# Weight tiles of 1056 words in place of 1040, and a constant of 64 words in place of 48, in a two-block transformer kernel

## The chip, the cores and the metric

The kernel runs on one core of one Trainium2 chip. The metric is device time in microseconds (us) of one execution, the median of several runs. The core has a matrix engine (PE, with a separate record PEld for its weight loads), a vector engine (DVE), a scalar engine (ACT), a general engine (POOL) and an engine that issues DMAs (SP).

## The reference

Two transformer blocks over 256 tokens of 2048 features, all in 32-bit floating point. What takes the time are the products with weight matrices; the attentions, norms and the modulation stand between them.

```
def first_block(x, ...):
    h = rmsnorm(x, pre_mix_g[l])
    proj = h @ w_in[l]                       # 2048 x 4368
    ...                                      # windowed and forgetting attention
    mix = concatenate([o_a, o_b]) @ w_out[l] # 2048 x 2048
    x = x + rmsnorm(mix, post_mix_g[l])
    u = causal_dwconv(rmsnorm(x, pre_ffn_g[l]) @ w_up[l], conv_w[l], conv_b[l])  # 2048 x 11264
    gate, val = split(u, 2)
    y = (gelu(gate) * val) @ w_down[l]       # 5632 x 2048
    x = x + rmsnorm(y, post_ffn_g[l])

def second_block(x, c, ctx, ...):
    ...                                      # modulation: silu(c) @ w_ada, 2048 x 12288
    q, k, v, u = split_projection(h @ w_in)  # 2048 x 2560; keys and values of ctx too
    x = x + g_a * (concatenate([attn, pool]) @ w_out)
    x = x + g_m * (square(relu(hm @ w_mlp_up)) @ w_mlp_down)  # 2048 x 8192 and back
    return rms_norm(x, final_norm_w)
```

## The kernel before

Every product streams its weight matrix once from memory. `run` walks over blocks of two weight tiles. A raw tile of 32-bit words arrives by DMA (`raw`), ACT rounds it into a tile `hi` (L156), and DVE subtracts to get the remainder `lo` (L168). The resident operand (x^T, features on partitions) lies in memory as `hi` and `lo` parts too, in tiles of the pools `a8` (names a8_...) and `p4` (p4_...). Each product of a weight tile and an x^T tile is made of three matmuls on the rounded 32-bit type: hi with hi, hi with lo, lo with hi.

`products` (the matmul is at L285) knows two forms. In form A the weights are the stationary operand (128 columns of them, loaded ahead of the matmul) and x^T is the moving one, 256 columns. In form B it is the other way round: 128 columns of x^T are stationary and 512 columns of the weights move (352 or 336 in the product `v`, 256 in part of `kv` and `ckv`). Form A makes up, mup, qk, qa, q, kva and half of kv and ckv: 9120 matmuls of 256 columns. Form B makes dn, mdn, wo_a, wo_b, wo2_p, wo2_a and u: 3552 matmuls of 512 columns. The product v (288) and the rest of kv and ckv (192) complete the 13152 matmuls of L285. A **unit** here is the work on one weight tile of 1024 words: 8 feature tiles of 3 matmuls in form A (24), 4 of 3 in form B (12). In a profile row, a name like b_up<-a,hi says: result bank of product up, moving operand from pool a8, stationary operand hi.

The weight tiles come from the pool `w`, four buffers for `hi` and four for `lo`. All tiles lie in one address space of bytes per partition, one pool after the other; the constants (pool `cst`) lie ahead of `raw`, `w`, `a8`, `p4`, `row` and `p2`. The width of 1040 words is set by the product v, the widest. A weight tile of 1040 words takes 4160 bytes, which is 32.5 times 128, so buffers alternate between starts that are multiples of 128 bytes and starts 64 bytes past one. The constant `heads` takes 192 bytes (1.5 times 128), after which everything starts 64 bytes past a multiple of 128. In the built program the first bytes are these (the remainder mod 256 in brackets; slices inside a tile are multiples of 512 bytes in form A and B, so they change nothing in it):

```
                     before                                  after
hi, in order of use  63424 [192] 75904 [128] 71744 [64] 67584 [0]    63488 [0] 76160 [128] 71936 [0] 67712 [128]
lo, in order of use  80064 [192] 92544 [128] 88384 [64] 84224 [0]    80384 [0] 93056 [128] 88832 [0] 84608 [128]
a8 (eight of 8192)   96704 [192], all eight [192]                    97280 [0], all eight [0]
p4 (nine of 4096)    162240 [192], all nine [192]                    162816 [0], all nine [0]
```

Of the kernel before, what the change touches and what calls it, by code (L numbers as in the profile page):

```python
# [9 lines left out]
F32R = mybir.dt.float32r  # L10
# [4 lines left out]
D = 2048  # L15
T = 256
# [5 lines left out]
# columns of the packed per-feature vectors  # L22
# [9 lines left out]
# when the adaptive modulation takes a step, by product: every so many ticks (99: never), or at these ticks  # L32
# [4 lines left out]
# products without a reader while the norms before these products run  # L37
# [3 lines left out]
class Group:  # L41
    """One weight-streaming product: blocks of two 128-row weight tiles against a resident x^T."""
# [10 lines left out]
def a_banks(nf, col0=0):  # L53
    """Feature-major results: two 128-feature tiles of 256 tokens per bank."""
    return [[("A", 256 * j, col0 + 128 * (i + j)) for j in range(min(2, nf - i))] for i in range(0, nf, 2)]


def b_banks(widths, col0=0):
    """Token-major results: one bank per token tile and column chunk."""
    out = []  # L60
    for tt in range(2):
        c = col0
        for n in widths:
            out.append([("B", 0, n, tt, c)])
            c += n
    return out


class Kernel:
# [51 lines left out]
    def run(self, groups):  # L121
        nc = self.nc
        blocks = [(g, b) for g in groups for b in range(g.nb)]
# [24 lines left out]
        def hi_to(j):  # L148
            while len(his) <= min(j, 2 * len(blocks) - 1):
                dma_to(len(his) // 2 + 2)  # L150
                views, raw, w = part(len(his))
                self.n += 1
                hi = self.w_p.tile([128, 1040], F32R, tag="hi", name=f"hi{self.n}")[:, :w]
                with self.behind("hi"):
                    for h, r in views(hi, raw):
                        nc.scalar.copy(h, r)  # L156
                his.append(hi)

        def lo_to(j):
            while len(los) <= min(j, 2 * len(blocks) - 1):  # L160
                n = len(los)
                hi_to(n)
                views, raw, w = part(n)
                self.n += 1
                lo = self.w_p.tile([128, 1040], F32R, tag="lo", name=f"lo{self.n}")[:, :w]
                with self.behind("lo"):
                    for (l, r), (h, _) in zip(views(lo, raw), views(his[n], raw)):
                        self.dve.tensor_tensor(out=l, in0=r, in1=h.bitcast(F32), op=ALU.subtract)  # L168
                los.append(lo)

        banks = None
        for i, (g, b) in enumerate(blocks):
# [40 lines left out]
            if g.tail and b == g.nb - 2:  # L213
                # the first token tile's results come before the second's
                w2 = []
                for u in range(4):
                    lo_to(2 * i + u)
                    hi_to(2 * i + 3)
                    w2.append((his[2 * i + u], los[2 * i + u]))
                    for n in range(nb // 2):  # L220
                        unit(banks[n], g.banks[n], u)
                    self.tick(False)
                for n in range(nb):
                    if n >= nb // 2:
                        for u in range(4):
                            unit(banks[n], g.banks[n], u)
                    mm = self.mm
                    g.done(n, banks[n])
                continue
# [38 lines left out]
    def behind(self, kind):  # L268
        """Issue order after an instruction of a norm that the next products wait for."""
        q = self.held[kind]  # L270
        return self.tc.issue_after(q.pop(0).ins) if q else nullcontext()
# [31 lines left out]
    def later(self, *steps, every=1):  # L303
        """Run steps one by one at coming ticks."""
        def gen():
            for f in steps:
                for _ in range(every):
                    yield
                f()
        self.sides.append(gen())  # L310

    def keep_warm(self, n, after=None, rhs=None):
        """Products without a reader, so that the tensor engine's clock stays up while it would wait."""
        bk = self.bank("warm")
        rhs = self.vecs[:, 0:512] if rhs is None else rhs
        with self.tc.issue_after(after.ins) if after else nullcontext():
            for _ in range(n):
                self.nc.tensor.matmul(bk[:, 0:rhs.shape[-1]], self.ones, rhs, start=True, stop=True, skip_group_check=True)

    def preload(self, func, after):  # L320
        """Has the scalar engine load the table of a function ahead of its use."""
# [9 lines left out]
    def loader(self, w, k0, c0, n):  # L331
        """Blocks of two k-tiles from row k0 and columns c0:c0+n."""
# [7 lines left out]
    def make_ht(self, src, gain, shift=None):  # L340
        """src(tt, k) -> token-major [128, 128]; gain, shift: per-feature columns."""
# [40 lines left out]
        def head(tt):  # L382
            """The first four k-tiles of one token tile."""
# [18 lines left out]
    def rstd(self, parts, n):  # L402
        """(mean of squares + eps) ** -0.5 from partial sums [128, m]."""
# [14 lines left out]
    def scale_rows(self, x, ss, n=D, out=None, first=False):  # L418
        """x * rstd for a token tile; the first of two on one engine, else shared by two."""
# [12 lines left out]
    def row(self, src):  # L432
        """A vector of D on every partition, in two tiles; returns columns of it."""
# [6 lines left out]
    def attn1(self, jobs, v_of, evac, bias, sink):  # L440
        """jobs: (q, k, j, half, head). Yields once per head."""
# [87 lines left out]
    def o_evac(self, his, los, gain, acc, base=0):  # L529
        """o^T of a head pair: times the group's gain, split, and its squares summed."""  # L530
# [16 lines left out]
    def token_rstd(self, acc, n):  # L547
        """rstd per token [128, 2] from squares summed feature-major [128, 256]."""
# [49 lines left out]
    def row_of(self, cols, tile_=None):  # L598
        """A [128, 2048] tile whose every row is the vector held in columns [128, 16]."""
# [13 lines left out]
    def main(self):  # L613
# [15 lines left out]
        heads = self.const("heads", [128, 48])  # L629
# [29 lines left out]
        # x^T of the first block, one token tile after the other  # L659
# [19 lines left out]
        def silu_rows():  # L679
            """silu of c and c_ctx, each along every partition's row."""  # L680
# [18 lines left out]
        # -- v and forget gates, token-major  # L699
# [63 lines left out]
        # -- k and v of the windowed heads  # L763
# [16 lines left out]
        # -- q of the windowed heads, heads j and j + 8 in one tile  # L780
# [19 lines left out]
        # -- q and k of the forgetting heads, with the windowed attention beside them  # L800
# [27 lines left out]
        # -- output projection: windowed heads, then forgetting heads  # L828
        w_out = a["w_out"]

        def pair_rows(w, r0, n, c0):
            """Rows of k-tile j: 64 of head j, 64 of head j + n, among 2n heads from row r0."""
# [28 lines left out]
        def residual(y, x, r):  # L861
            """x += y * r for one token tile; returns the squares' sums of the new x."""
# [8 lines left out]
        def add_norm(n, half, y, hold):  # L871
            """One result chunk of y: its squares, its gain, and then x += norm(y) and y = norm(x)."""
# [44 lines left out]
        # -- residual + norm, then x^T of the next product  # L917
# [6 lines left out]
        # -- first feed-forward  # L924
# [79 lines left out]
        # context: norm, modulation and its x^T beside the last products  # L1004
# [39 lines left out]
        # -- second block: context keys and values  # L1044
# [9 lines left out]
        def split(x, his, lo):  # L1054
            """hi + lo of x [128, 512], hi by partition halves in two tiles."""
# [5 lines left out]
        def twice(c):  # L1061
            """The high parts of the keys in the other partition half too."""
# [6 lines left out]
        # -- second block: projections of the latent tokens  # L1069
# [20 lines left out]
        def rope(x, his, lo):  # L1090
            """Rotated x [128, 512] (features on partitions, 256 tokens twice), as hi (by halves in two tiles) + lo."""
# [33 lines left out]
        # -- attention over the latent window and the context  # L1125
        def attn2():
            # per half s of the heads: high parts in their own partitions, low parts in the other half
# [141 lines left out]
        # -- output projection of the second block: x += g_a * (...)  # L1269
# [51 lines left out]
        # -- second feed-forward  # L1321
# [27 lines left out]
        def finish(n, half):  # L1349
            """The gain of one chunk of the last norm, and the norm when a token tile is complete."""  # L1350
# [77 lines left out]
def arrays(inp):  # L1428
    """The inputs as the program takes them, and constants that depend on shapes alone."""
# [10 lines left out]
    # the two halves of w's columns c0:c1, side by side by 512  # L1440
# [59 lines left out]
```

## Time and profile before

| | us |
|---|---|
| median of 3 runs | 2158.41 |
| lowest and highest run | 2158.36, 2160.49 |
| span of the profiled execution, first to last instruction | 2159.2 |
| PE busy in it | 2134.7 (99%) |
| PEld busy | 1926.6 (89%) |
| DVE busy | 1578.7 (73%) |
| ACT busy | 1076.4 (50%) |

The span is the profiled execution's own time; it lies 0.8 us above the median of the runs. A matmul's recorded duration reaches over the start of the next one, since matmuls are pipelined; the time that one costs in a stream is the step from its start to the start of the next, and that is read from the starts of rows.

### The profile page before, as it was taken

The page shows a single profiled execution, that of the slowest core. Times are in us where ns is not written, and L with a number is a line of the kernel's source. Part 1 is how long each engine was busy: PE and PEld are TensorE (multiplying, and loading weights), DVE is VectorE, ACT ScalarE, POOL GpSimd, SP SyncE. Part 2 cuts the span into 40 slices and gives each one's busy share as a digit, 9 for nine tenths or more (in the row PEclk, how much of TensorE's full clock was granted, in tenths as well). Part 3 has the DMA queues.
Part 4 walks back from the last instruction along what each step waited for, and adds up shares of the span by engine and source line. Part 5 has one row for each costly group of instructions (what it writes and reads, how often), then busy time and mean ns, then how long its engine had stood idle before and what let it go on. Part 6 is the DMA issues. An engine that isn't in the chain of part 4 may idle for free.

```text
span 2159.2 us, 35018 instructions
## 1 busy us (share of the span) xinstructions
PE 2134.7 (99%) x14342; PEld 1926.6 (89%) x14342; DVE 1578.7 (73%) x2094; ACT 1076.4 (50%) x1557; POOL 38.3 (2%) x58
## 2 busy tenths in 40 slices
PE   8999999999999999999999999999999999999998
PEld 7988877999998999989889878889898998989986
DVE  6777688888689787887899777765656657555476
ACT  5456565555454543544666466354543434434343
POOL 0001010000000000000000000000000000000000
PEclk9999999999999999999999999999999999999999
DMA  8753675667767788787878744855767677565572
GB/s 309 262 191 123 157 230 218 231 244 248 254 216 254 252 298 309 273 310 255 307 259 287 247 139 156 196 175 177 252 200 270 215 246 243 191 194 179 194 233 98
DMA packets 120640, 490.86 MB, mean 227 GB/s; under 512 B 8672, under 2 KB 12576, under 8 KB 107040
## 3 DMA queue, kind: packets, MB, share of 16 engines
q1 hardware_dynamic: 120480, 488.63, 67.0%
q8 instruction: 112, 1.84, 0.3%
q14 instruction: 48, 0.39, 0.0%
HBM read 484.90 MB, written 2.13 MB: 226 GB/s over the span
## 4 chain that ended last, share of the span: by engine, by line
PE 95%; DVE 2%; ACT 1%; DMA 1%; POOL 0%; issue 0%; POOLq 0%; ACTq 0%; SPq 0%; DVEq 0%
PE b_up L285 23%; PE b_mup L285 17%; PE b_mdn L285 16%; PE b_dn L285 11%; PE b_qk L285 4%; PE b_wo_a L285 4%; PE b_u L285 2%; PE b_v L285 2%; PE b_wo_p L285 2%; PE b_qa L285 2%; PE b_q L285 2%; PE b_wo_b L285 2%; PE b_aux L1156 1%; PE b_aux L1199 1%; PE b_aux L1185 1%; PE b_aux L495 1%
## 5 line engine op out<-in xcount | busy, mean ns | idle before, releaser
L168 DVE TENSOR_TENSOR lo<-raw,hi 128x1024 fp32r<-128x1024 f32 (+2 forms) x716 | 850.0, 1198 | 445.7 <-ACT hi L156 444.2
L156 ACT CAST hi<-raw 128x1024 fp32r<-128x1024 f32 (+2 forms) x716 | 729.7, 1029 | 859.8 <-PE b_up L285 218.9
L285 PE MATMUL b_up<-a,hi 128*128 128x256 f32 x2816 | 493.9, 280 | 0.0
L285 PEld LDWEIGHTS b_up<-a,hi 128*128 128x128 f32 x2816 | 430.8, 189 | 0.4
L285 PE MATMUL b_up<-a,lo 128*128 128x256 f32 x1408 | 392.8, 279 | 0.0
L285 PE MATMUL b_mup<-a,hi 128*128 128x256 f32 x2048 | 358.8, 279 | 1.3 <-ACT a L370 1.3
L285 PE MATMUL b_mdn<-hi,p 128*128 128x512 f32 x1024 | 319.9, 393 | 0.0
L285 PEld LDWEIGHTS b_mup<-a,hi 128*128 128x128 f32 x2048 | 312.8, 189 | 2.1 <-ACT a L370 1.6
L285 PE MATMUL b_mup<-a,lo 128*128 128x256 f32 x1024 | 285.4, 279 | 0.0
L285 PEld LDWEIGHTS b_up<-a,lo 128*128 128x128 f32 x1408 | 266.1, 189 | 0.0
L583 DVE SCALAR_TENSOR_TENSOR raw<-raw,srow 128x2048 f32<-128x2048 f32 x96 | 219.4, 2286 | 28.5 <-DMA raw<-in_w_ada 28.3
L285 PEld LDWEIGHTS b_mdn<-hi,p 128*128 128x128 f32 x1024 | 191.7, 188 | 44.2
L285 PE MATMUL b_dn<-hi,p 128*128 128x512 f32 x704 | 220.1, 394 | 0.0
L285 PE MATMUL b_mdn<-lo,p 128*128 128x512 f32 x512 | 201.3, 393 | 0.0
L285 PEld LDWEIGHTS b_mup<-a,lo 128*128 128x128 f32 x1024 | 193.4, 189 | 0.0
L285 PEld LDWEIGHTS b_dn<-hi,p 128*128 128x128 f32 x704 | 131.5, 188 | 30.1
L285 PE MATMUL b_dn<-lo,p 128*128 128x512 f32 x352 | 138.5, 393 | 0.0
L285 PEld LDWEIGHTS b_mdn<-lo,p 128*128 128x128 f32 x512 | 96.3, 188 | 22.2
L285 PE MATMUL b_qk<-a,hi 128*128 128x256 f32 x512 | 94.0, 285 | 0.0
L285 PE MATMUL b_wo_a<-hi,a 128*128 128x512 f32 x256 | 81.1, 398 | 0.0
L285 PEld LDWEIGHTS b_qk<-a,hi 128*128 128x128 f32 x512 | 78.2, 189 | 2.6 <-issue 2.0
L285 PEld LDWEIGHTS b_dn<-lo,p 128*128 128x128 f32 x352 | 66.2, 188 | 15.6 <-DVE lo L168 0.4
(264 smaller groups left out, 2542.0 us busy)
## 6 DMA issues: line engine op xcount, KB each, us to landing
raw<-in_w_ada SPq DMA_DIRECT2D x96, 1024.0 KB, 5.6
raw<-in_w_up SPq DMA_DIRECT2D x88, 1024.0 KB, 5.0
raw<-in_w_mlp_up SPq DMA_DIRECT2D x64, 1024.0 KB, 5.1
raw<-in_w_mlp_down SPq DMA_DIRECT2D x64, 1024.0 KB, 5.7
raw<-in_w_in SPq DMA_DIRECT2D x50, 1024.0 KB, 6.0
raw<-in_w_down SPq DMA_DIRECT2D x44, 1024.0 KB, 6.2
raw<-in_w_out SPq DMA_DIRECT2D x32, 512.0 KB, 6.8
raw<-in_w_out SPq DMA_DIRECT2D x16, 1024.0 KB, 6.1
```

Source lines behind the costliest of these rows:

```text
L156: nc.scalar.copy(h, r)
L168: self.dve.tensor_tensor(out=l, in0=r, in1=h.bitcast(F32), op=ALU.subtract)
L285: self.mm = self.pe.matmul(dst, lhsT, rhs, start=first and n == 0 and m == 0, stop=last and n == len(prog) - 1 and m == 2, skip_group_chec ...
L495: self.pe.transpose(t[:, 128 * m:128 * m + 128], z[:, 1 + 128 * m:129 + 128 * m], self.ident)
L583: self.dve.scalar_tensor_tensor(out=r, in0=r, scalar=1.0, in1=self.srow[0], op0=ALU.mult, op1=ALU.mult, accum_out=self.ada[:, f:f + 1])
L1156: self.pe.matmul(bk[:, 256 * m:256 * m + 256], x, k[:, 512 * m + o:512 * m + o + 256], start=n == 0 and m == 0, stop=n == 1 and m == 1, sk ...
L1185: self.pe.transpose(bk[:, 128 * m:128 * m + 128], z[:, 128 * m:128 * m + 128], self.ident)
L1199: self.pe.matmul(o[64 * s:64 * s + 64, 128 * qt:128 * qt + 128], v[:, c:c + 64], PT[x][:, 128 * kt:128 * kt + 128], start=kt == 0, stop=kt ...
```

## The change

The tiles hi and lo become 1056 words wide (4224 bytes, 33 times 128), of which the same columns are used as before. The constant heads becomes 64 words wide, of which 48 are used. By this every hi and lo buffer and every tile of a8 and p4 begins at a multiple of 128 bytes. No instruction is added, removed or moved on any engine: the orders of the five engines are the same row by row, and so are the shapes. Only start addresses differ. (Comments were taken out besides.)

```
-                hi = self.w_p.tile([128, 1040], F32R, tag="hi", name=f"hi{self.n}")[:, :w]
+                hi = self.w_p.tile([128, 1056], F32R, tag="hi", name=f"hi{self.n}")[:, :w]
...
-                lo = self.w_p.tile([128, 1040], F32R, tag="lo", name=f"lo{self.n}")[:, :w]
+                lo = self.w_p.tile([128, 1056], F32R, tag="lo", name=f"lo{self.n}")[:, :w]
...
-        heads = self.const("heads", [128, 48])
+        heads = self.const("heads", [128, 64])[:, 0:48]
```

## Rows read from the trace of the kernel before

**Rows 1.** The page: busy time by engine, and the clock in 40 slices.

```profile
PE 2134.7 (99%) x14342; PEld 1926.6 (89%) x14342; DVE 1578.7 (73%) x2094; ACT 1076.4 (50%) x1557; POOL 38.3 (2%) x58
...
PEclk9999999999999999999999999999999999999999
```

**Rows 2.** The page: the chain that ended last, share of the span by engine.

```profile
PE 95%; DVE 2%; ACT 1%; DMA 1%; POOL 0%; issue 0%; POOLq 0%; ACTq 0%; SPq 0%; DVEq 0%
```

**Rows 3.** Stretches of up5, dn21, mdn20, qk0, u: length, busy time (x) by engine, PEclk.

```profile
core 0: us, PE busy (x) PEld busy (x) DVE busy (x) ACT busy (x) POOL busy (x), PEclk, DMA share, GB/s
692.20:736.80 44.60, 44.60 (x384) 44.56 (x383) 30.70 (x34) 21.01 (x28) 0.54 (x1) 1.00 0.71 256
670.00:692.00 22.00, 22.00 (x97) 17.84 (x96) 19.03 (x21) 8.08 (x9) 0.00 (x0) 1.00 0.83 302
1702.90:1724.90 22.00, 22.00 (x98) 17.86 (x97) 18.04 (x20) 10.28 (x13) 0.00 (x0) 1.00 0.70 226
122.50:192.80 70.30, 70.30 (x532) 60.44 (x531) 53.74 (x128) 40.11 (x100) 9.23 (x16) 1.00 0.42 143
1215.10:1303.90 88.80, 88.80 (x513) 66.71 (x513) 73.31 (x175) 53.02 (x114) 0.00 (x0) 1.00 0.51 160
```

**Rows 4.** Timeline of PE in up5, form A: start, length, instruction, count.

```profile
714.58 0.40 PE L285 MATMUL b_up<-a,hi 128*128 128x256 f32 x2
714.82 0.28 PE L285 MATMUL b_up<-a,lo 128*128 128x256 f32 x1
714.94 0.40 PE L285 MATMUL b_up<-a,hi 128*128 128x256 f32 x2
...
717.46 0.39 PE L285 MATMUL b_up<-a,hi 128*128 128x256 f32 x2
...
717.80 0.39 PE L285 MATMUL b_up<-a,hi 128*128 128x256 f32 x2
...
720.18 0.39 PE L285 MATMUL b_up<-a,hi 128*128 128x256 f32 x2
...
723.02 0.40 PE L285 MATMUL b_up<-a,hi 128*128 128x256 f32 x2
...
725.76 0.40 PE L285 MATMUL b_up<-a,hi 128*128 128x256 f32 x2
```

**Rows 5.** Timeline of PE in mdn20, form B, same columns.

```profile
1702.88 0.63 PE L285 MATMUL b_mdn<-hi,p 128*128 128x512 f32 x2
...
1705.63 0.63 PE L285 MATMUL b_mdn<-hi,p 128*128 128x512 f32 x2
...
1708.43 0.62 PE L285 MATMUL b_mdn<-hi,p 128*128 128x512 f32 x2
...
1711.22 0.62 PE L285 MATMUL b_mdn<-hi,p 128*128 128x512 f32 x2
...
1713.97 0.63 PE L285 MATMUL b_mdn<-hi,p 128*128 128x512 f32 x2
```

**Rows 6.** Timeline of PE in kv, both forms from one weight tile, same columns.

```profile
1149.27 0.40 PE L285 MATMUL b_kv<-hi,a 128*128 128x256 f32 x2
...
1149.62 0.40 PE L285 MATMUL b_kv<-hi,a 128*128 128x256 f32 x2
...
1155.07 0.39 PE L285 MATMUL b_kv<-a,hi 128*128 128x256 f32 x2
...
1155.41 0.39 PE L285 MATMUL b_kv<-hi,a 128*128 128x256 f32 x2
...
1155.76 0.39 PE L285 MATMUL b_kv<-hi,a 128*128 128x256 f32 x2
...
1156.10 0.39 PE L285 MATMUL b_kv<-hi,a 128*128 128x256 f32 x2
...
1156.43 0.39 PE L285 MATMUL b_kv<-hi,a 128*128 128x256 f32 x2
```

**Rows 7.** Timeline of PE: transposes and a product on unrounded words, same columns.

```profile
1156.78 1.03 PE L353 MATMUL b_aux<-ident,a 128*128 128x128 f32 x8
...
1311.48 7.07 PE L1258 MATMUL b_aux<-p,a 128*128 128x256 f32 x32
```

**Rows 8.** Durations of single instructions at L353 and L1258: count, min/median/max in ns.

```profile
L353 PE MATMUL b_aux<-ident,a x120: 270/272/421, 22.3 to 1463.1; 128*128 128x128 f32 x120
...
L1258 PE MATMUL b_aux<-p,a x32: 379/379/379, 1311.5 to 1318.2; 128*128 128x256 f32 x32
```

## The prediction

> **What bounds the kernel now.** I read the busy times first, then the chain of waits, then the stretches, then the starts of single matmuls. PE is busy for 2134.7 of 2159.2 us and its clock is granted in full (2.4 GHz) in every slice [rows 1]. The chain that ended last is PE for 95% of the span [rows 2]. In the streaming stretches PE never stops, while DVE works for 69 to 87% of the time and ACT for less than half; only the attention stretches qk0 and u come near a limit of DVE (54 of 70 and 73 of 89 us) [rows 3]. So the time is the number of matmuls times the step from one start to the next, and only what changes a step counts. Busy times and durations of single matmuls don't show the step, since they overlap; the starts do.
>
> **What the steps show.** In up5 (form A) four weight tiles follow each other, and the x^T tiles all begin 192 bytes past a multiple of 256. The units of 24 matmuls start at 714.58, 717.46, 720.18, 723.02 and 725.76, so they take 2.88, 2.72, 2.84 and 2.74 us, 11.18 us for the four [rows 4]. Nothing else than the buffers' start addresses follows this pattern: the weights begin at 192, 128, 64 and 0 mod 256 in this order. The two long units have stationary operands that begin 64 bytes past a multiple of 128, the two short ones aligned ones. A step is 120, 113, 118 and 114 ns. In form B (mdn20) the x^T tile is stationary, always off by 64, and the moving weights alternate; the units of 12 start at 1702.88, 1705.63, 1708.43, 1711.22 and 1713.97, so they take 2.75, 2.80, 2.79 and 2.75 us for weights at 192, 128, 64 and 0 [rows 5]. Whether the moving operand is aligned makes no difference of note there (2.775 aligned, 2.77 not).
>
> **Two readings of the same rows.** Before the change x^T is never aligned to 128, so two rules fit form A alike. By the first, each operand's own start counts: a stationary operand at a multiple of 128 is faster. By the second, the distance of the two operands counts: when weights and x^T start an odd multiple of 64 bytes apart the two streams of reads fit between each other, and when they start an even multiple apart (0 or 128 mod 256) they collide. After the change every distance is 0 or 128 mod 256, half of the units each, as in the two long units now; and every start is aligned, as in half of the short units now. The first rule makes the kernel faster and the second makes it slower, by nearly the same amount.
>
> What decides for me is three things. First, the two long units differ, 2.88 at distance 0 and 2.84 at distance 128 [rows 4], though their stationary operands have the same start mod 128; an own start mod 128 can't do this, a distance can. Second, kv works on one weight tile in both forms. With weights at 0 its form A steps (x^T moving) take 0.34 us per three matmuls (1155.07 to 1155.41), and form B, in which the misaligned x^T is now the stationary operand, has steps of 0.34 and 0.33 just behind (1155.76 to 1156.10 to 1156.43) [rows 6]. By a rule on the stationary operand alone these should be the 0.36 of the long units. The distance is odd in both. Third, in form B the moving operand's start does nothing [rows 5], where a rule of own starts with a price for each operand would show it. Against it: another unit of kv has form B steps of 0.35 at an odd distance (1149.27 to 1149.62) [rows 6], so the distance is not all; and no row has both operands aligned.
>
> At this place a rule of the Trainium skill speaks against both readings. TensorE: Matmul & The Clock Gate, section Step-by-step: what each phase is for, says that PE has two independent read ports, one for the moving operand and one for LDWEIGHTS, and that loading the next weights doesn't steal read bandwidth from the running matmul. By that rule the place of the operands would be free and the sum of this change zero, 2159 us. The trace disagrees: units alike in all but addresses take 2.88 and 2.72 us [rows 4].
>
> **The sum, by the distance.**
> - Form A: 9120 matmuls are 380 units. The mean unit now is 11.18/4 = 2.795 us. After, half have distance 0 and half 128: (2.88 + 2.84)/2 = 2.86 us. 380 x 0.065 = +24.7 us.
> - Form B of 512 columns: 3552 matmuls are 296 units. Now (2.75 + 2.80 + 2.79 + 2.75)/4 = 2.773; after, distances 0 and 128: (2.75 + 2.79)/2 = 2.77. That is -0.9 us.
> - The product v (288 matmuls) and form B of kv and ckv (192): at most 0.007 us each, the difference of 120 and 113 ns, half of them odd now: below 2 us; taken as +0.3.
> - ACT and DVE read and write the moved tiles, DMAs land in moved raw tiles. Counted at nothing: PE hides them, with DVE at 19.03 of 22.00 us in the fullest stretch of dn and 30.70 of 44.60 in up [rows 3]. If PE got an eighth faster in dn, DVE's conversion of the weights would end last there, and this cover would be gone. No wait is added and no queue is passed.
> Sum: 2159.2 + 24.7 - 0.9 + 0.3 = 2183.3 for the profiled execution, which lies 0.8 above the median: **2182 us**. Bounds of this case alone: if all units ran like 2.84, 2176; if all like 2.88, 2191; its own range is 2175 to 2192.
>
> **The rivals.**
> 1. *Own starts count; faster.* For it speaks that both short units have aligned stationary operands [rows 4]. The sure part would be the long units becoming short: (2.86 - 2.73) x 190 = -24.7 us, 2134. If form B gains as much for each stationary operand (0.13/24 = 5.4 ns) x 3552 = -19 us more, 2115. If the moving operand's alignment helps as well there is a floor. Eight transposes, each a weight load and 128 columns, take 1.03 us [rows 7] with 0.27 for the last one [rows 8], so (1.03 - 0.27)/7 = 109 ns each, the pace of weight loads alone; in form A that makes 24 x 0.109 = 2.61 per unit, -70 us. The product at L1258, on unrounded words, takes (7.07 - 0.38)/31 = 216 ns for 256 columns [rows 7, 8]; these run at half the pace, so 512 columns without any extra would take that, against 2.773/12 = 231 in form B: -54 us. Both floors together give 2159 - 124 = 2035. I put this rival's middle at 2115. It decides as soon as a unit with both operands at 0 takes 2.73 or less.
> 2. *It changes nothing that can be measured*: the aligned pair gives form A a step between the two, or form A loses what form B wins (+25 and -19 as above); 2155 to 2163.
> 3. *DVE becomes the bound*: only behind rival 1. In qk0 and u DVE is busy for 76% and 83% [rows 3], so about 3 us of what rival 1 gives there would be lost. It changes no sign.
>
> **How the numbers follow.** Distances decide: 0.50, at 2182. Own starts decide: 0.40, of which 0.28 between 2085 and 2140 and 0.12 below 2085, towards the floors. No change: 0.10. The bound of what a measurement of this kernel can tell from no change is 0.2%, 4.3 us. Faster 0.40, same 0.10, slower 0.50. The range must reach over to the other sign: 2085 to 2192 leaves out the 0.12 below and some 0.03 above.
>
> **What would show it.** In the changed kernel the starts in up5 tell all: if every unit of 24 takes 2.84 to 2.88 us, distance decides and the kernel is slower; if every one takes 2.73 or less, own starts decide. In mdn20 the units stay at 2.75 to 2.79 by the first, and fall to about 2.7 by the second. Wrong would be the whole argument if up5 had long and short units still, or if b_dn's units changed and b_up's did not. The order of work, DVE's and ACT's durations and the waits should be as before in each case.

## The result: 2182.0 us, one per cent slower, and the profile after

The changed kernel takes 2182.03 us (median of 4 runs, 2181.54 to 2182.55), the kernel before 2159.12 beside it (4 runs, 2158.36 to 2160.49). The ratio is 1.0103, with a 95% interval of 1.0089 to 1.0117. The forecast was 2182.0, slower.

The page of the changed kernel, busy times, clock, chain, and the groups of line, operation and tile (busy us, mean ns of one, idle before):

```profile
PE 2156.0 (99%) x14342; PEld 1950.0 (89%) x14342; DVE 1580.6 (72%) x2094; ACT 1077.0 (49%) x1557; POOL 40.0 (2%) x58
...
PEclk9999999999999999999999999999999999999999
...
PE 96%; DVE 1%; ACT 1%; DMA 1%; issue 0%; POOL 0%; POOLq 0%; ACTq 0%; SPq 0%; DVEq 0%
...
L168 DVE TENSOR_TENSOR lo<-raw,hi 128x1024 fp32r<-128x1024 f32 (+2 forms) x716 | 850.9, 1199 | 469.2 <-ACT hi L156 467.1
...
L156 ACT CAST hi<-raw 128x1024 fp32r<-128x1024 f32 (+2 forms) x716 | 729.8, 1029 | 885.2 <-PE b_up L285 222.8
...
L285 PE MATMUL b_up<-a,hi 128*128 128x256 f32 x2816 | 505.6, 283 | 0.0
...
L285 PE MATMUL b_mdn<-hi,p 128*128 128x512 f32 x1024 | 319.2, 393 | 0.0
```

These answer to [rows 1, 2]. PE is still busy for all but 1% of the span, its clock is still granted in full in every slice, and the chain is PE for 96%. DVE's and ACT's conversions take what they took, 1199 and 1029 ns here, 1198 and 1029 before:

```profile
L168 DVE TENSOR_TENSOR lo<-raw,hi 128x1024 fp32r<-128x1024 f32 (+2 forms) x716 | 850.0, 1198 | 445.7 <-ACT hi L156 444.2
...
L156 ACT CAST hi<-raw 128x1024 fp32r<-128x1024 f32 (+2 forms) x716 | 729.7, 1029 | 859.8 <-PE b_up L285 218.9
```

So nothing new ends last: the same matmuls follow each other at a longer step. The timeline of PE in up5, form A, first matmul of each unit (start, length, instruction, count), answers to [rows 4]:

```profile
699.27 0.39 PE L285 MATMUL b_up<-a,hi 128*128 128x256 f32 x2
...
702.13 0.39 PE L285 MATMUL b_up<-a,hi 128*128 128x256 f32 x2
...
704.97 0.40 PE L285 MATMUL b_up<-a,hi 128*128 128x256 f32 x2
...
707.85 0.39 PE L285 MATMUL b_up<-a,hi 128*128 128x256 f32 x2
...
710.69 0.40 PE L285 MATMUL b_up<-a,hi 128*128 128x256 f32 x2
```

The units take 2.86, 2.84, 2.88 and 2.84 us; before they took 2.88, 2.72, 2.84 and 2.74. The first of the five starts lies just behind a matmul of another product; from the second on the two lengths alternate, as the distances 0 and 128 do. No short unit is left. In mdn20, form B, the same view answers to [rows 5]:

```profile
1720.72 0.63 PE L285 MATMUL b_mdn<-hi,p 128*128 128x512 f32 x2
...
1723.47 0.62 PE L285 MATMUL b_mdn<-hi,p 128*128 128x512 f32 x2
...
1726.26 0.63 PE L285 MATMUL b_mdn<-hi,p 128*128 128x512 f32 x2
...
1728.99 0.62 PE L285 MATMUL b_mdn<-hi,p 128*128 128x512 f32 x2
...
1731.79 0.39 PE L285 MATMUL b_mdn<-hi,p 128*128 128x512 f32 x1
```

These units take 2.75, 2.79, 2.73 and 2.80 us, on average 2.768 against 2.773: hardly anything moved there. The two lengths belong to the distances here too, 2.75 and 2.73 at 0, 2.79 and 2.80 at 128.

For a sum over the whole kernel, the mean step from the start of one matmul to the next can be worked out from all starts in a trace. It is taken here over all matmuls of L285, without the few that are followed by a stop (steps of 0.4 us and more). In ns, for some kernels that come below as well:

| kernel | form A, 256 columns (9120) | form B, 512 (3552) | form B, 256 (192) | v (288) |
|---|---|---|---|---|
| before | 117.3 | 233.2 | 118.7 | 166.1 |
| changed | 120.0 | 232.6 | 119.5 | 165.4 |
| e1, x^T 64 past | 114.9 | 232.5 | 117.2 | 164.7 |
| e5, x^T 32 past | 118.1 | 235.2 | 119.4 | 163.4 |
| e6, x^T 96 past | 120.0 | 234.9 | 118.1 | 166.4 |
| e7, x^T hi and lo apart | 119.2 | 232.7 | 118.4 | 162.7 |

From before to the changed kernel: form A 9120 x 2.7 = +24.6 us, form B 3552 x -0.6 = -2.1, the two small ones -0.05 together. That is +22.5; the spans differ by 2180.6 - 2159.2 = +21.4.

With the start addresses of the built program beside the steps, the kernel before shows the pattern of [rows 4] over the whole of form A: 120.9 ns at distance 0, 118.8 at 128, 114.2 at 64 and 114.6 at 192, some 2270 matmuls each.

### The profile page after: what moved, and what is told of

Same layout as the page of the kernel before. It is cut to its first block, busy times and chain, and to the rows that moved or that the text cites. A ratio compares the mean times of both kernels' runs of the same rounds, so it can differ in the third digit from the quotient of the medians.

```text
span 2180.6 us, 35018 instructions
## 1 busy us (share of the span) xinstructions
PE 2156.0 (99%) x14342; PEld 1950.0 (89%) x14342; DVE 1580.6 (72%) x2094; ACT 1077.0 (49%) x1557; POOL 40.0 (2%) x58
## 4 chain that ended last, share of the span: by engine, by line
PE 96%; DVE 1%; ACT 1%; DMA 1%; issue 0%; POOL 0%; POOLq 0%; ACTq 0%; SPq 0%; DVEq 0%
PE b_up L285 23%; PE b_mup L285 17%; PE b_mdn L285 16%; PE b_dn L285 10%; PE b_qk L285 4%; PE b_wo_a L285 4%; PE b_u L285 2%; PE b_v L285 2%; PE b_q L285 2%; PE b_qa L285 2%; PE b_wo_p L285 2%; PE b_wo_b L285 2%; PE b_aux L1156 1%; PE b_ckv L285 1%; PE b_kv L285 1%; PE b_aux L1199 1%
## 5 line engine op out<-in xcount | busy, mean ns | idle before, releaser
L168 DVE TENSOR_TENSOR lo<-raw,hi 128x1024 fp32r<-128x1024 f32 (+2 forms) x716 | 850.9, 1199 | 469.2 <-ACT hi L156 467.1
L156 ACT CAST hi<-raw 128x1024 fp32r<-128x1024 f32 (+2 forms) x716 | 729.8, 1029 | 885.2 <-PE b_up L285 222.8
L285 PE MATMUL b_up<-a,hi 128*128 128x256 f32 x2816 | 505.6, 283 | 0.0
L285 PEld LDWEIGHTS b_up<-a,hi 128*128 128x128 f32 x2816 | 436.7, 190 | 0.5
L285 PE MATMUL b_up<-a,lo 128*128 128x256 f32 x1408 | 397.7, 282 | 0.0
L285 PE MATMUL b_mup<-a,hi 128*128 128x256 f32 x2048 | 367.2, 282 | 1.3 <-ACT a L370 1.3
L285 PE MATMUL b_mdn<-hi,p 128*128 128x512 f32 x1024 | 319.2, 393 | 0.0
L285 PEld LDWEIGHTS b_mup<-a,hi 128*128 128x128 f32 x2048 | 317.0, 190 | 2.1 <-ACT a L370 1.6
L285 PE MATMUL b_mup<-a,lo 128*128 128x256 f32 x1024 | 288.9, 282 | 0.0
L285 PEld LDWEIGHTS b_up<-a,lo 128*128 128x128 f32 x1408 | 268.0, 190 | 0.0
L285 PEld LDWEIGHTS b_mdn<-hi,p 128*128 128x128 f32 x1024 | 191.7, 188 | 43.8
L285 PE MATMUL b_dn<-hi,p 128*128 128x512 f32 x704 | 219.7, 393 | 0.0
L285 PE MATMUL b_mdn<-lo,p 128*128 128x512 f32 x512 | 201.2, 393 | 0.0
L285 PEld LDWEIGHTS b_mup<-a,lo 128*128 128x128 f32 x1024 | 194.6, 190 | 0.0
L285 PEld LDWEIGHTS b_dn<-hi,p 128*128 128x128 f32 x704 | 131.6, 188 | 29.7
L285 PE MATMUL b_dn<-lo,p 128*128 128x512 f32 x352 | 138.4, 393 | 0.2 <-DVE lo L168 0.2
L285 PEld LDWEIGHTS b_mdn<-lo,p 128*128 128x128 f32 x512 | 96.0, 188 | 22.0
L285 PE MATMUL b_qk<-a,hi 128*128 128x256 f32 x512 | 95.2, 287 | 0.0
L285 PEld LDWEIGHTS b_qk<-a,hi 128*128 128x128 f32 x512 | 78.8, 189 | 2.6 <-issue 2.0
L285 PE MATMUL b_wo_a<-hi,a 128*128 128x512 f32 x256 | 81.0, 397 | 0.0
L285 PEld LDWEIGHTS b_dn<-lo,p 128*128 128x128 f32 x352 | 66.1, 188 | 15.7 <-DVE lo L168 0.6
```

Source lines behind the costliest of these rows:

```text
L285: self.mm = self.pe.matmul(dst, lhsT, rhs, start=first and n == 0 and m == 0, stop=last and n == len(prog) - 1 and m == 2, skip_group_chec ...
```

## The experiments

The theory, "distance": the start of an x^T tile less the start of a weight tile, mod 256, decides; 0 and 128 make form A slow, 64 and 192 make it fast. The rival, "own starts": an operand that begins at a multiple of 128 is better in itself (and something else cost the changed kernel its gain). A pad below is a tile of its own that nobody uses; it only shifts what lies behind it. All diffs are against the changed kernel. The first four ran beside the kernel before at 2160.21 us (13 runs), the other three beside 2159.92 (7 runs).

**e1: weights at multiples of 128, x^T moved by 64.**

```
-        self.w_p = P("w", 4)
+        self.w_p = P("w", 4); P("pad_w", 1).tile([128, 16], F32, tag="pad_w", name="pad_w")
```

> Weight tiles begin at multiples of 128 bytes, all x^T tiles 64 bytes past one, so every distance of the two operands is an odd multiple of 64 (64 or 192 mod 256). Theory distance: every form A unit takes 2.72 to 2.74 us, as the short units of the kernel before; 380 x (2.86 - 2.73) = 49 us less than the changed kernel's 2182, so 2133; form B stays within 3 us. Rival own starts (a stationary operand off 128 costs, and after the changed kernel's result a moving x^T at a multiple of 128 costs too): 2133 as well. Rival that only a mixture of buffers runs well (short units because they follow long ones): between 2158 and 2182.

Measured: 2135.65 us (4 runs, 2133.16 to 2136.11), ratio to before 0.9887 [0.9872, 0.9902]. The timeline of PE in up5, first matmul of each unit:

```profile
687.35 0.40 PE L285 MATMUL b_up<-a,hi 128*128 128x256 f32 x2
...
690.09 0.39 PE L285 MATMUL b_up<-a,hi 128*128 128x256 f32 x2
...
692.80 0.39 PE L285 MATMUL b_up<-a,hi 128*128 128x256 f32 x2
...
695.52 0.39 PE L285 MATMUL b_up<-a,hi 128*128 128x256 f32 x2
...
698.25 0.39 PE L285 MATMUL b_up<-a,hi 128*128 128x256 f32 x2
```

Every unit is short now, 2.74, 2.71, 2.72 and 2.73 us. A pad of 64 bytes that nobody reads turned +1.0% into -1.1%, and this kernel is faster than both. The page shows what else changed with it:

```profile
PE 2109.6 (99%) x14342; PEld 1904.2 (89%) x14342; DVE 1576.4 (74%) x2094; ACT 1079.3 (51%) x1557; POOL 39.3 (2%) x58
...
L168 DVE TENSOR_TENSOR lo<-raw,hi 128x1024 fp32r<-128x1024 f32 (+2 forms) x716 | 850.0, 1200 | 404.0 <-ACT hi L156 402.9
...
L156 ACT CAST hi<-raw 128x1024 fp32r<-128x1024 f32 (+2 forms) x716 | 731.7, 1032 | 807.3 <-PE b_up L285 195.0
...
PE 94%; DVE 2%; DMA 1%; ACT 1%; issue 1%; POOL 0%; POOLq 0%; ACTq 0%; SPq 0%; DVEq 0%
```

PE's busy time falls by 46 us against the changed kernel; the conversions stay at 1200 and 1032 ns. What ends last is still PE, for 94% of the chain.

**e2: the other way round, weights 64 past a multiple of 128, x^T at one.** A 16-word pad as in e1 stands behind `raw` and another behind `w`.

```
-        self.raw_p = P("raw", 4)
+        self.raw_p = P("raw", 4); P("pad_raw", 1).tile([128, 16], F32, tag="pad_raw", name="pad_raw")
...
-        self.w_p = P("w", 4)
+        self.w_p = P("w", 4); P("pad_w", 1).tile([128, 16], F32, tag="pad_w", name="pad_w")
```

> The same distances with the places swapped: weight tiles 64 bytes past a multiple of 128, x^T tiles at multiples of 128. Theory distance: short units throughout, 2133. Rival own starts: the stationary weights are off 128 and the moving x^T is at a multiple of 128, both of which cost by it, so units of 2.86 or more and 2182 or more. The two are 49 us apart.

Measured: 2135.09 us (4 runs, 2134.48 to 2136.33), 0.9887 [0.9873, 0.9902]. The same view of up5:

```profile
687.25 0.40 PE L285 MATMUL b_up<-a,hi 128*128 128x256 f32 x2
...
689.99 0.39 PE L285 MATMUL b_up<-a,hi 128*128 128x256 f32 x2
...
692.71 0.39 PE L285 MATMUL b_up<-a,hi 128*128 128x256 f32 x2
...
695.43 0.39 PE L285 MATMUL b_up<-a,hi 128*128 128x256 f32 x2
```

All units are short again, with every stationary operand off by 64. In the kernel before, stationary operands like these stood in the two long units. By own starts this kernel could not be faster than the changed one. That rival falls here.

**e3: both moved by 64.** Tiles of 1056 words, and the narrow constant of before.

```
-        heads = self.const("heads", [128, 64])[:, 0:48]
+        heads = self.const("heads", [128, 48])
```

> The wider weight tiles alone, the constant left at 48 words: weights and x^T all begin 64 bytes past a multiple of 128, distances 0 and 128 as in the changed kernel, starts all other. Theory distance: 2182, equal to the changed kernel within 3 us, units of 2.88 and 2.84 in turn. Rival own starts: the moving x^T off 128 is the better place for it, the stationary weights off 128 the worse, so it need not equal the changed kernel; by the rows of before the long units stay and it lies at 2182 only by chance; if each operand's start mattered for itself, a difference over 10 us to the changed kernel would be seen.

Measured: 2181.87 us (4 runs, 2181.25 to 2182.78), 1.0104 [1.0087, 1.0121]; the changed kernel to within 0.2 us. In up5:

```profile
703.78 0.40 PE L285 MATMUL b_up<-a,hi 128*128 128x256 f32 x2
...
706.66 0.39 PE L285 MATMUL b_up<-a,hi 128*128 128x256 f32 x2
...
709.50 0.40 PE L285 MATMUL b_up<-a,hi 128*128 128x256 f32 x2
...
712.38 0.39 PE L285 MATMUL b_up<-a,hi 128*128 128x256 f32 x2
```

The units are 2.88, 2.84 and 2.88 as in the changed kernel, though no operand of these units begins at a multiple of 128. With it all four pairs of places have been run, weights and x^T each at a multiple of 128 or 64 past one: the two with like places take 2182 us, the two with unlike ones 2135.

**e4: the wider constant alone, weight tiles of 1040 words.** The x^T tiles begin at multiples of 256, the weights at 0, 192, 128 and 64 in order of use.

```
-                hi = self.w_p.tile([128, 1056], F32R, tag="hi", name=f"hi{self.n}")[:, :w]
+                hi = self.w_p.tile([128, 1040], F32R, tag="hi", name=f"hi{self.n}")[:, :w]
```

and the same for `lo`.

> The wider constant alone, weight tiles left at 1040 words: x^T at multiples of 128, weight buffers alternate between 0 and 64 past, distances 0, 64, 128, 192 in turn as in the kernel before. Theory distance: 2158, as the kernel before, with units of about 2.88, 2.72, 2.84, 2.74, but now the units with aligned weights are the long ones. Rival own starts (moving x^T at a multiple of 128 costs): all units long, 2182.

Measured: 2160.42 us (10 runs, 2158.41 to 2162.57), 1.0002 [0.9992, 1.0011]. In up5:

```profile
689.73 0.41 PE L285 MATMUL b_up<-a,hi 128*128 128x256 f32 x2
...
692.60 0.39 PE L285 MATMUL b_up<-a,hi 128*128 128x256 f32 x2
...
695.33 0.39 PE L285 MATMUL b_up<-a,hi 128*128 128x256 f32 x2
...
698.16 0.40 PE L285 MATMUL b_up<-a,hi 128*128 128x256 f32 x2
...
700.90 0.40 PE L285 MATMUL b_up<-a,hi 128*128 128x256 f32 x2
```

Long and short alternate as in the kernel before (2.87, 2.73, 2.83, 2.74), but the long ones are now those with aligned weights: their distances are 0 and 128. In [rows 4] the long ones had the weights that were off by 64. The parity of the distance stayed with the length, the alignment did not.

**e5 and e6: distances between.** The pad of e1 with 8 words (x^T 32 bytes past; distances of 32 and 160) and with 24 (96 past; 96 and 224).

```
-        self.w_p = P("w", 4)
+        self.w_p = P("w", 4); P("pad_w", 1).tile([128, 8], F32, tag="pad_w", name="pad_w")
```

> Weight tiles at multiples of 128 bytes, x^T tiles 32 bytes past one: distances 32 and 160 mod 256. It asks how fine the distance is felt. If memory is read in pieces of 64 bytes, half of each piece of one stream falls on a collision with the other: units between 2.73 and 2.86, some 2.80, and a time between 2135 and 2182, about 2158. If the pieces are 32 bytes or less, a distance of 32 is as good as 64: 2135. If only the first piece of each operand counts (both starts lie in the same 64 bytes), 2182.

> The same with x^T 96 bytes past a multiple of 128: distances 96 and 224 mod 256. By the same three cases: about 2158 (half a collision), 2135 (fine pieces), or, if only the piece of the start counts, 2135 too, since 96 lies in the odd piece of 64 bytes. So with the run at 32 the three cases give 2158 and 2158, 2135 and 2135, 2182 and 2135.

Measured: e5 2173.11 us (4 runs, 2171.85 to 2174.65), 1.0065 [1.005, 1.008]; e6 2189.45 us (4 runs, 2187.34 to 2191.21), 1.0137 [1.012, 1.0154]. In up5, e5:

```profile
697.52 0.40 PE L285 MATMUL b_up<-a,hi 128*128 128x256 f32 x2
...
700.33 0.40 PE L285 MATMUL b_up<-a,hi 128*128 128x256 f32 x2
...
703.13 0.40 PE L285 MATMUL b_up<-a,hi 128*128 128x256 f32 x2
...
705.95 0.40 PE L285 MATMUL b_up<-a,hi 128*128 128x256 f32 x2
```

and e6:

```profile
704.08 0.40 PE L285 MATMUL b_up<-a,hi 128*128 128x256 f32 x2
...
706.92 0.40 PE L285 MATMUL b_up<-a,hi 128*128 128x256 f32 x2
...
709.80 0.40 PE L285 MATMUL b_up<-a,hi 128*128 128x256 f32 x2
...
712.64 0.40 PE L285 MATMUL b_up<-a,hi 128*128 128x256 f32 x2
```

Units of 2.80 to 2.82 us in e5 and 2.84 to 2.88 in e6. None of the expected cases meets either time. If two streams were read in pieces of 64 bytes, or if the cost rose and fell evenly between the bad and the good distance, 32 and 96 should be alike. They are not: form A steps by 118.1 ns at 32 and 160, and by 120.0 at 96 and 224, which is as bad as 0 and 128. And form B, which the other shifts hardly touched, pays here: 235.2 and 234.9 ns against 233.2, so 3552 x 2.0 = +7.1 and 3552 x 1.7 = +6.0 us. With form A (9120 x 0.8 = +7.3 and 9120 x 2.7 = +24.6) the sums are +14.4 and +30.6; the spans grew by 12.2 (2171.4) and 30.2 (2189.4). So e6 is slower than the changed kernel by its form B, not by its form A.

**e7: the hi and lo parts of x^T at different parities.** The x^T tiles of `a8` become 8256 bytes apart, so that the hi and the lo part no longer begin at the same place mod 256. In most products one part then lies at an even distance (0 or 128) and the other at an odd one (64 or 192). In the first half of the features of `mup` both lie at odd ones, which the expectation, with one or two of the three matmuls odd, left out.

```
-        return self.a8_p.tile(shape, dt, tag="a8", name=f"a8_{self.n}")
+        t = self.a8_p.tile([128, 2064], dt, tag="a8", name=f"a8_{self.n}")[:, :2048]; return t if len(shape) == 2 else t.rearrange("p (k t) -> p k t", t=shape[2])
```

> The changed kernel with 64 bytes behind each a8 tile, so that the hi and the lo part of x^T in form A lie at distances of different parity to the same weight tile: of the three matmuls (hi, hi), (hi, lo), (lo, hi) either one or two have an odd distance. If each pair of a stationary and a moving operand is felt by itself, a unit takes 24 times the mean of 119 and 113.7 in that share: 2.77 or 2.81 us, and the steps inside differ. If the tile as a whole, or the first pair of a unit, sets the pace, units are 2.73 or 2.86. The whole kernel: 2149 or 2166 by the first, 2135 or 2182 by the second.

Measured: one run, 2174.64 us, span 2172.9. In up5:

```profile
699.62 0.40 PE L285 MATMUL b_up<-a,hi 128*128 128x256 f32 x2
...
702.48 0.40 PE L285 MATMUL b_up<-a,hi 128*128 128x256 f32 x2
...
705.32 0.40 PE L285 MATMUL b_up<-a,hi 128*128 128x256 f32 x2
...
708.18 0.40 PE L285 MATMUL b_up<-a,hi 128*128 128x256 f32 x2
```

Units of 2.86, 2.84 and 2.86 us, and 119.2 ns a step: nearly all of the gain is gone, though 64% of form A's matmuls have an odd distance. If each pair of operands had a price of its own, form A would have stepped by some 116.7 ns (an estimate: 120.0 less 0.64 of the 5.1 down to 114.9). Nor does the gain come back where every pair is odd. In the first half of `mup`, with distances of 64 and 192 alone, first matmul of each unit:

```profile
1490.22 0.40 PE L285 MATMUL b_mup<-a,hi 128*128 128x256 f32 x2
...
1493.05 0.40 PE L285 MATMUL b_mup<-a,hi 128*128 128x256 f32 x2
...
1495.88 0.40 PE L285 MATMUL b_mup<-a,hi 128*128 128x256 f32 x2
...
1498.70 0.40 PE L285 MATMUL b_mup<-a,hi 128*128 128x256 f32 x2
...
1501.53 0.40 PE L285 MATMUL b_mup<-a,hi 128*128 128x256 f32 x2
```

Units of 2.83, 2.83, 2.82 and 2.83 us. By the starts, this half of `mup` steps by 118.0 ns, where `mup` as a whole steps by 113.9 in e1 and by 119.3 in the changed kernel. In e7 the share of odd distances hardly counts: 118.3 ns with a third of them odd (the other half of `mup`), 118.8 with two thirds (up1 to up9), 118.0 with all. So an odd distance of each pair is not enough. What e1 and e2 have besides, and e7 has not, is that both parts of x^T begin at the same place mod 256, so that one distance holds all through a unit. Whether that is the condition, and why, these runs don't tell.

## Why the prediction was right, point by point

- **What bounds the kernel: right.** PE ends last in every kernel that was run (94 to 97% of the chain), and the time moved with the step alone. Between the changed kernel and e1 the step of form A differs by 5.1 ns; 9120 x 5.1 = 46.5 us, and the spans differ by 2180.6 - 2134.2 = 46.4.
- **Distance or own starts: right, at 0.50 against 0.40, and the runs made it sure.** The two readings gave one and the same pattern in [rows 4], so the trace of before could hardly tell them apart; what decided, the 2.88 against 2.84 of two units with the same start mod 128, was a sound hint. e3 moves both operands and nothing happens; e1 and e2 move one or the other and both gain the same; e4 turns the alignment round and the pattern stays with the distance. All these kernels have both parts of x^T at the same place mod 256, as the kernels before and after the change have; e7 shows that without it the reading by distance fails. The range of 2085 to 2192 held both signs, so it was the lengths of the units that put the forecast to the test.
- **Form A, +24.7 us: right.** 9120 x 2.7 ns = +24.6. The units of 2.88 and 2.84 came in turn as forecast.
- **Form B, -0.9 us: right in kind, a little more in size.** -0.6 ns a step make -2.1 us.
- **v, kv and ckv, +0.3: too small to see,** -0.05 by the table. That kv also had 0.35 us steps at an odd distance [rows 6] was put against the theory. The table bears the doubt out: form B of 256 columns gains less from the odd distance (119.5 to 117.2 ns in e1) than form A (120.0 to 114.9), so kv, the second of the prediction's three hints, was a weak one.
- **The cover: held.** DVE's and ACT's instructions take what they took, and even in e1, where PE is faster, PE ends last. The third rival, DVE as the next bound, had nothing to bite on: e1 gains 25.0 us of span against before, and the steps alone make 9120 x 2.4 + 3552 x 0.7 + 192 x 1.5 + 288 x 1.4 = 25.1.
- **The sum** was 2183.3 for the span, 2.7 too high (form B and v some 1.6 of it by the table). That the median came out exact is luck: a second small error went the other way. The profile of the changed kernel was taken in an execution of 2182.39 us, 1.8 above its span. The prediction took the span of before as 0.8 above its median; with 1.8 outside the span that execution would have taken some 2161.0 (an estimate), about 1.9 more than the median of its runs. The bounds of 2176 and 2191 are spans as well; less the same 0.8 they would be 2175 and 2190.
- **No change, at 0.10:** an aligned pair steps like the long units of before, not between long and short, and form B doesn't balance form A.
- **The rule that stood against it.** By the Trainium skill, TensorE: Matmul & The Clock Gate, section Step-by-step: what each phase is for, the moving operand and the weight load have read ports of their own, and a load takes no read bandwidth from the running matmul. What the prediction drew from it, that the place of the operands is free, the runs contradict: 2135.65 and 2182.03 us with the same instructions. Whether the ports are what collides, they don't show.

That the two streams of reads collide, as the prediction put it, was only argued. Shown is that the distance of the starts decides, as long as both parts of x^T begin at the same place mod 256. A collision of pieces of 64 bytes in the simple form that stood behind the expectations of e5 and e6 doesn't fit their times, and a price for each pair doesn't fit e7. What happens inside stays open. Distances below 64 bytes other than 32 were not tried.

## What to carry to other kernels

In a stream of matmuls on rounded 32-bit words, with a weight load for each and 256 columns, look at the distance of the two operands' starts mod 128, not at each one's alignment: with 64 the whole kernel took 2.1% less time here than with 0. Where an operand comes in parts, as hi and lo, keep the parts at the same place mod 256, since e7 lost the gain without it. Where units of equal work take different times in turn, list the start addresses of both operands beside the units; if two rules fit, one pad in front of one operand tells them apart. The best version here is the changed kernel with a pad of 64 bytes per partition between weights and x^T; e2 takes the same time within its spread.

## What the runs showed of the hardware that was not expected

- An odd distance of every pair is not enough: in e7, with the two parts of x^T at 64 and 192, `mup` stepped by 118.0 ns, against 113.9 in e1, where both parts begin at the same place.
- 32 and 96 bytes are not alike: 118.1 and 120.0 ns for 256 columns, 2173.11 and 2189.45 us.
- With 512 moving columns, even or odd distance is worth next to nothing on the mean (232.6 and 232.5 ns), though 0 and 128 differ by 2.4 ns in the changed kernel (231.0 and 233.4); 32 and 96 cost 2 to 3 ns more than either mean (235.2 and 234.9).
